# Seven half products instead of eight quarters in both mixers' output projections of a two-layer hybrid decoder trunk

## The chip, the cores and the metric

One core of a Trainium2 chip. The metric is the device time of one execution in microseconds (us), the median of the runs.

## The reference, cut to what matters

512 tokens of 1024 features pass two residual layers; layer 0 mixes by causal pooling, layer 1 by dilated windowed attention. Each layer adds its mixer's output and then a gated feed-forward to the stream x. The part that changes is the last line of each mixer, a product of 512 x 1024 tokens with a 1024 x 1024 weight:

```python
def pool_mixer(h, w_in, w_group, scale, w_out):
    ...
    z = jnp.einsum('bsgc,gce->bsge', p, w_group).reshape(B, S, D_MODEL) * scale
    return jnp.einsum('bsd,de->bse', z, w_out)

def attn_mixer(h, w_qkv, w_out):
    ...
    return jnp.einsum('bse,ed->bsd', merged, w_out)

def reference(...):
    for i in range(DEPTH):
        ...
        x = x + y
        h = rmsnorm(x, norm_ffn[i])
        x = x + swiglu(h, ...)
    return rmsnorm(x, norm_final)
```

## The kernel before, in words

**Precision.** Every float32 operand is split into a high part (a cast to fp32r, done by ACT: whi, bhi, p_hi, h) and a low part (DVE subtracts the cast from the source: wlo, blo, p_lo, h). A product takes three matmuls: high x high, high x low, low x high.

**Weights.** `queue` is one list of all weight blocks in the order of their use. `weights(i)` (L151) loads ahead on SP's queue into the ring wraw, and casts (L171) and subtracts (L175) a few items ahead into whi and wlo, or bhi and blo for items with the pool "b". SP's loads wait, in order, for the splits that free their raw buffer. Items of the feed-forward can be sums of two blocks: the second block is added by an accumulating DMA that POOL issues (L138), or by DVE (L177). One form, "loads" (L180), adds a further block to a raw buffer right after that buffer was split, so that the next item is the running sum.

**Order.** PE's instructions are written in the order in which they run. On ACT, DVE, POOL and SP a scheduler orders them by priority, and `tc.high_priority(URGENT)` puts an instruction ahead. Each engine works through its own list in order, so an instruction that waits holds back all behind it.

**Layer 0.** The windows' matmuls (L562) make p from u in two halves; `group_products(half, banks)` (L570) multiplies p by the group weights, ACT scales the result into the high tokens z_hi (L582) and DVE makes z_lo (L583). `out_projection` (L415) is called once the first half of the groups is there; the second half, 24 matmuls, is a hook behind its first weight block.

**The projection.** Columns 0 to 511 first, in four weight blocks of 256 rows, each for four blocks of 128 tokens (the four banks `four`); then columns 512 to 1023, a token block at a time, with all four weights at hand: 192 matmuls of 128x512 (L425 to L427). Each finished bank is added to x (into_stream, L413's row in the profile), squared and summed by ACT, and multiplied by the next norm's gain, so that the norm of a token block is prepared while the next is multiplied. Before the last token block, blocks 0 and 1 are transposed (L366), and behind it block 2 (L358), for the feed-forward.

**Layer 1.** The attention's heads are merged per 128 features: `merged(t)`, t = 0 to 7, 12 to 24 small matmuls into one of the banks mm, then one DVE multiplication (L1338, L1342) with the heads' weights, which frees the bank, then a split into tokens m_hi, m_lo. The heads' weights come to LB and even_rows by DMAs on POOL's queue (L1250); LB is a ring of three, refilled for t = 5 to 7 when t = 0 to 2 are multiplied. Then the same projection follows.

**Feed-forward.** It already takes seven products per block, with sums of tokens (t1 to t4) and sums of weights; `PLAN` sets its steps.

Of the kernel before, what the change touches and what calls it, by code (L numbers as in the profile page):

```python
# [10 lines left out]
F32 = mybir.dt.float32  # L11
# [6 lines left out]
P = 128  # L18
S = 512
# [50 lines left out]
PLAN = _plan()  # L70
TOKENS = np.arange(S).reshape(J, R).T.reshape(-1)
# [4 lines left out]
def trunk_kernel(ctx: ExitStack, tc: tile.TileContext, x_in, xT, gam, gains, consts, ident_d, w0, wT, w1, wv, w_down, out):  # L76
# [49 lines left out]
    def load(i):  # L126
# [3 lines left out]
        raw = (pools["v"] if item["kind"] == "v" else wraw).tile([P, 1024], F32, name="vraw" if item["kind"] == "v" else "wraw")  # L130
# [20 lines left out]
    def weights(i, split_ahead=4, load_ahead=5, held=0):  # L151

        load_ahead = queue[i].get("ahead", load_ahead)
        for n in range(loaded["w"], min(len(queue), i + load_ahead)):
            if queue[n]["kind"] == "w":
                load(n)
            loaded["w"] = n + 1
        load_sums()
        while len(ready) < min(loaded["w"], i + split_ahead):
            item = queue[len(ready)]  # L160
            if item["kind"] == "v" and "v" not in pools:
                break
# [34 lines left out]
    w_out, wo = (rows_of(wT[i]) for i in range(2))  # L197
    j_grp = [enqueue(w0[8], (4, 2 * P))]
    j_out = [w_out(BY_GROUP[0], 0)]
    j_grp.append(enqueue(w0[9], (4, 2 * P)))  # L200
    j_out += [w_out(BY_GROUP[i], 0) for i in (2, 4, 6)] + [w_out(BY_GROUP[i], 1, pool="b") for i in (0, 2, 4, 6)]
# [58 lines left out]
    j_wo = [wo(2 * i, 0) for i in range(4)] + [wo(2 * i, 1, pool="b") for i in range(4)]  # L260
# [206 lines left out]

    with ExitStack() as pctx:
# [3 lines left out]
        early = [pmm.tile([P, S], F32, name=f"early{i}") for i in range(4)]  # L472
        p_hi, p_lo = (pm.tile([P, NC, S], F32R, name=name) for name in ("p_hi", "p_lo"))
# [96 lines left out]
        def group_products(half, banks):  # L570
            whi, wlo = weights(j_grp[half])
            for gg in range(2):
                g = 3 - (2 * half + gg)
                for m in range(2):
# [6 lines left out]
                    sc = g_sb[:, NC + e : NC + e + 1]  # L581
                    nc.scalar.activation(z_hi[:, e, :], ps, AF.Copy, scale=sc)  # L582
# [3 lines left out]

        for b in range(4):
            u_out(b, 0, early[b])
# [12 lines left out]
        banks = [early[0:2], early[2:4]]  # L601

        def turned_banks():
            return banks.pop(0)

        third = out_projection(j_out, BY_GROUP, z_hi, z_lo, norm, SHIFT, [mm.tile([P, S], F32, name="mm") for _ in range(4)], turned_banks, lambda: group_products(1, early))

    def ffn(layer, norm, third, nxt):
# [8 lines left out]
        with ExitStack() as fctx:  # L617
# [261 lines left out]
            for at, (kind, n, i, *zs) in enumerate(PLAN[:-4]):  # L879
                if at in (0, 2):  # L880
                    b = 2 + at // 2
                    if b == 2:
                        late_banks[b] = third
                        norm.prepare(3, COLS)
                    else:
# [100 lines left out]
    with ExitStack() as actx:  # L986
# [359 lines left out]
        for t in range(8):  # L1346
            cast, rest = merged(t)
# [81 lines left out]
```

## Time and profile before

| | us |
|---|---|
| median of 3 runs (lowest to highest) | 981.42 (980.79 to 981.96) |
| the profiled execution | 980.24 |
| its span, first to last instruction | 978.5 |
| layer 0's projection on PE, with 24 group products and the first transposes | 63.3 to 113.7 |
| layer 1's merged heads and projection on PE | 593 to 647.3 |

Engines: PE is TensorE's matmuls, PEld its weight loads, DVE, ACT, POOL, and SP, which issues loads. A row of a timeline gives start, length, engine, line, operation, out<-in, shape and count (x4: four in a row), and in brackets the idle time before it and what ended that. A row of groups gives count | busy us, mean ns of one | idle time before them. Neighbours on one engine overlap by some 0.1 us, so a queue moves a little faster than the means say.

### The profile page before, as it was taken

How to read it: one execution, taken by the hardware profiler on the slowest of the kernel's cores; microseconds unless marked ns; L12 is line 12 of the kernel's file. 1: busy time of each engine (PE TensorE's matmuls, PEld its weight loads, DVE VectorE, ACT ScalarE, POOL GpSimd, SP SyncE). 2: the span in 40 equal slices, each digit the busy share in tenths (PEclk: the TensorE clock that was granted, in tenths of full speed). 3: DMA queues.
4: the chain of work that ended last, by engine and by line, in shares of the span. 5: the costliest groups of instructions: out<-in, count | busy, mean ns of one | idle time of the engine just before them, and what ended most of it. 6: DMA issues, size and time to landing. Idle time of an engine off the chain costs nothing.

```text
span 978.5 us, 15597 instructions
## 1 busy us (share of the span) xinstructions
PE 970.9 (99%) x6028; PEld 862.6 (88%) x6028; DVE 783.9 (80%) x1083; ACT 575.3 (59%) x903; POOL 124.7 (13%) x124
## 2 busy tenths in 40 slices
PE   9999999999999999999999999999999999999997
PEld 8888899988988999889888899899998998899886
DVE  6475799888888888797897547579988898888876
ACT  6573566655665666574553554366664675567655
POOL 0002010010011111101212124101011101110110
PEclk9999999999999999999999999999999999999999
DMA  9448267479668877555221249627657947987652
GB/s 346 176 157 207 45 187 186 124 200 248 165 151 222 218 201 159 117 193 165 86 79 55 62 137 295 115 59 204 174 145 205 251 111 173 250 213 193 153 134 101
DMA packets 79466, 163.00 MB, mean 167 GB/s; under 512 B 6096, under 2 KB 6480, under 8 KB 79392
## 3 DMA queue, kind: packets, MB, share of 16 engines
q1 hardware_dynamic: 58544, 122.04, 37.6%
q0 software_dynamic: 20560, 39.69, 23.7%
q8 instruction: 47, 0.77, 0.3%
q14 instruction: 27, 0.22, 0.1%
q10 hardware_dynamic: 288, 0.27, 0.1%
HBM read 159.85 MB, written 2.13 MB: 166 GB/s over the span
## 4 chain that ended last, share of the span: by engine, by line
PE 99%; ACT 0%; DVE 0%; issue 0%; ACTq 0%
PE pair L703 32%; PE pair L847 21%; PE p L729 5%; PE mm L264 5%; PE mm L266 4%; PE mm L265 4%; PE pair L729 4%; PE r L729 2%; PE early L515 2%; PE mm L425 2%; PE mm L427 2%; PE mm L426 2%; PE mm L729 1%; PE mm L1297 1%; PE mm L1298 1%; PE mm L1299 1%
## 5 line engine op out<-in xcount | busy, mean ns | idle before, releaser
L175 DVE TENSOR_TENSOR wlo<-wraw,whi 128x1024 fp32r<-128x1024 f32 (+2 forms) x190 | 221.7, 1172 | 65.6 <-ACT whi L171 65.0
L171 ACT CAST whi<-wraw 128x1024 fp32r<-128x1024 f32 (+2 forms) x189 | 184.0, 979 | 138.4 <-PE pair L703 27.8
L171 ACT CAST whi<-vraw 128x1024 fp32r<-128x1024 f32 (+1 forms) x108 | 105.2, 980 | 117.6 <-DVE vraw L177 39.8
L175 DVE TENSOR_TENSOR wlo<-vraw,whi 128x1024 fp32r<-128x1024 f32 (+1 forms) x108 | 121.5, 1133 | 46.2 <-ACT whi L171 46.2
L703 PE MATMUL pair<-h,whi 128*128 128x512 f32 (+1 forms) x640 | 143.2, 349 | 0.0
L703 PEld LDWEIGHTS pair<-h,whi 128*128 128x128 f32 x640 | 109.1, 188 | 13.4
L703 PE MATMUL pair<-t,whi 128*128 128x512 f32 (+1 forms) x512 | 110.6, 337 | 0.0
L847 PE MATMUL pair<-whi,u_hi 128*128 128x512 f32 (+1 forms) x284 | 109.9, 387 | 0.0
L847 PE MATMUL pair<-wlo,u_hi 128*128 128x512 f32 (+1 forms) x284 | 109.9, 387 | 0.0
L847 PE MATMUL pair<-whi,u_lo 128*128 128x512 f32 (+1 forms) x284 | 109.7, 386 | 0.0
L703 PEld LDWEIGHTS pair<-t,whi 128*128 128x128 f32 x512 | 86.1, 190 | 8.4
L703 PE MATMUL pair<-h,wlo 128*128 128x256 f32 x512 | 89.2, 281 | 0.0
L703 PEld LDWEIGHTS pair<-h,wlo 128*128 128x128 f32 x512 | 76.1, 188 | 4.2
L138 POOL DMA_DIRECT2D wraw<-w x22 | 26.6, 1211 | 396.0 <-DMA wraw<-w 123.2
L177 DVE TENSOR_TENSOR vraw<-vraw,wraw 128x1024 f32<-128x1024 f32 (+1 forms) x66 | 75.2, 1139 | 0.7
L703 PE MATMUL pair<-t,wlo 128*128 128x256 f32 x384 | 71.9, 282 | 0.0
L264 PE MATMUL mm<-h,whi 128*128 128x512 f32 (+1 forms) x176 | 64.3, 365 | 0.0
L266 PE MATMUL mm<-h,wlo 128*128 128x512 f32 (+1 forms) x176 | 63.4, 360 | 0.0
L265 PE MATMUL mm<-h,whi 128*128 128x512 f32 (+1 forms) x176 | 63.4, 360 | 0.0
L847 PEld LDWEIGHTS pair<-whi,u_lo 128*128 128x128 f32 x284 | 53.3, 188 | 10.9
L847 PEld LDWEIGHTS pair<-whi,u_hi 128*128 128x128 f32 x284 | 53.4, 188 | 10.4
L847 PEld LDWEIGHTS pair<-wlo,u_hi 128*128 128x128 f32 x284 | 53.4, 188 | 10.2
(363 smaller groups left out, 2021.4 us busy)
## 6 DMA issues: line engine op xcount, KB each, us to landing
wraw<-w SPq DMA_DIRECT2D x116, 512.0 KB, 4.7
wraw<-w_down SPq DMA_DIRECT2D x32, 512.0 KB, 4.2
vraw<-w SPq DMA_DIRECT2D x22, 512.0 KB, 4.8
wraw<-w POOLq DMA_DIRECT2D x22, 512.0 KB, 6.9
vraw<-w POOLq DMA_DIRECT2D x22, 512.0 KB, 9.1
wraw<-wT SPq DMA_DIRECT2D x16, 512.0 KB, 4.4
vraw<-w_down POOLq DMA_DIRECT2D x12, 512.0 KB, 6.5
wraw<-w_down SPq DMA_DIRECT2D x24, 256.0 KB, 3.3
```

What stands on the lines that cost most here:

```text
L138: nc.gpsimd.dma_start(dst, more, accum_op=ALU.add)
L171: nc.scalar.copy(hi[:, :n], raw[:, :n])
L175: nc.vector.tensor_sub(lo[:, :n], raw[:, :n], hi[:, :n].bitcast(F32))
L177: nc.vector.tensor_add(raws[into][:, :n], raws[into][:, :n], raws[more][:, :n])
L264: nc.tensor.matmul(ps, lhsT=whi, rhs=xhi, start=first, stop=False, **kw)
L265: nc.tensor.matmul(ps, lhsT=whi, rhs=xlo, start=False, stop=False, **kw)
L266: nc.tensor.matmul(ps, lhsT=wlo, rhs=xhi, start=False, stop=last, **kw)
L425: nc.tensor.matmul(ps, lhsT=xhi, rhs=w[0][:, k, :], start=first, stop=False)
L426: nc.tensor.matmul(ps, lhsT=xhi, rhs=w[1][:, k, :], start=False, stop=False)
L703: mat = lambda o, w, m, **kw: nc.tensor.matmul(o, lhsT=w, rhs=m, skip_group_check=True, **kw)
L729: nc.tensor.matmul(ps[:, g, :], lhsT=w[:, g, c, :], rhs=right[:, z, c, :], start=i in (0, 1, 3) and g + c + k == 0, stop=c == 3 and k == 2 ...
L847: nc.tensor.matmul(acc(t), lhsT=u, rhs=w, start=first, stop=n == len(places) - 1, skip_group_check=True)
```

## The change

`out_projection` stays in the code; both layers now call `seven_projection`. The tokens are taken as two halves of 256, the weight as 2 x 2 blocks of 512 x 512, and seven products of half the tokens with 512 x 512 weights replace eight: 7 x 24 matmuls of 128x512 instead of 192. They run in the order 0, 1, 2, 5, 4, 3, 6, each in two halves z of the rows.

Weights are 14 items instead of 8: products 0, 3 and 6 take one block, product 4 the sum of two, product 1 the sum of two in a buffer of its own pool "s" (sraw), and products 2 and 5 the same buffer after one further "loads" each (L188 after the change). The 14 are split like the 8 before.

Tokens: `Left` keeps the unsplit tokens (raw, two tiles) and one sum (spare), and splits seven operands ("places") of 128x1024: `first` for product 0, `second` for product 1, `behind` for the others, ahead of what they are used by, all URGENT. In layer 0 product 0's banks are copied by ACT (keep) and product 0 is not added to x by itself.

The feed-forward now transposes block 2 after its first step instead of finding it done. In layer 1 the first feed-forward weights are no longer tied behind the last split of the merged heads, and bhi, blo have 3 buffers instead of 4.

```diff
 def load(i):
+        if item.get("sums"):
+            raw = pools["s"].tile([P, 1024], F32, name="sraw")
+        else: ...

+    def enqueue_seven(w, order, then=None):
+        by = w.rearrange("(k p) c -> p k c", p=P)
+        js = {}
+        for i in SEVEN:
+            for z in range(2):
+                block = lambda m, k: by[:, order[2 * k + z] : order[2 * k + z] + 2, COLS[m]]
+                src = {0: [(0, 0)], 1: [(1, 0), (1, 1)], 3: [(0, 1)], 4: [(0, 0), (1, 0)], 6: [(1, 1)]}.get(i)
+                item = dict(kind="w" if src else "sum", shape=(2, S), rows=True, ahead=8, **({"pool": "b"} if z else {}))
...
+                    item["into"] = js[1][z]
+                if i == 1:
+                    item["sums"] = True
+                if i in (1, 2):
+                    item["loads"] = (js[1][z] if i == 2 else len(queue), block(0, i - 1))

+        def behind(self, i):
+            t, more = self.raw
+            with tc.high_priority(URGENT):
+                if i is None:
+                    self.next_sum(FIRST)
+                    self.split(2, self.spare)
+                    self.split(5, more[:, :, FIRST])
+                    nc.vector.tensor_sub(t[:, :, FIRST], more[:, :, FIRST], t[:, :, FIRST])
+                elif i == 0:
+                    self.split(6, t[:, :, FIRST])
+                elif i == 1:
+                    self.split(3, more[:, :, SECOND])
+                    self.next_sum(SECOND)
+                elif i == 4:
+                    self.split(4, self.spare)

+    def seven_projection(js, left, norm, shift, p, r, q, tps, after_first, keep):
+        accs = {0: p, 1: r, 2: p, 3: q, 4: p, 5: r, 6: p}
+        def operands(i):
+            return [weights(j, split_ahead=6, held=z + (i in (4, 3, 6))) for z, j in enumerate(js[i])]
...
+        products(0, operands(0))
+        after_first()
+        left.behind(0)
...
+        product(1)
+        product(2)
+        product(5)
+        for b in range(2):
+            norm.square(b, 0)
+            norm.gained(b, 0)
+        left.reserve()
+        product(4)
...
+            norm.prepare(b)
+        product(3)
...
+        rests = turned_rows(norm, shift, list(enumerate(tps())))
+        ws = operands(6)
+        rests()
...

 # group_products, layer 0
+                        with tc.high_priority(URGENT):
+                            nc.scalar.activation(raw[half][:, 2 * gg + m, :], ps, AF.Copy, scale=sc)
+                            if half == 0 and m == 1:
+                                left.first(2 * gg)
+                        continue

+            def after_first():
+                group_products(1, early)
+                left.second()
+                left.behind(None)

 # merged(t), layer 1
+                with tc.high_priority(URGENT):
+                    if t in (1, 3):
+                        left.first(t - 1)
+                    elif t == 4:
+                        left.second()
+                    elif t == 7:
+                        left.behind(None)
```

DVE in layer 0, from the second half of product 0's weights on. Before: the low parts of the four blocks of columns 512 to 1023 (blo), then of a weight block, and z_lo of the second groups (L583, out h).

```order
L175 TENSOR_TENSOR blo<-wraw,bhi 128x1024 x4
L175 TENSOR_TENSOR wlo<-wraw,whi 128x1024
L583 SCALAR_TENSOR_TENSOR h<-early_102,g_sb,h 128x512
L583 SCALAR_TENSOR_TENSOR h<-early_103,g_sb,h 128x512
L583 SCALAR_TENSOR_TENSOR h<-early_104,g_sb,h 128x512
L175 TENSOR_TENSOR wlo<-wraw,whi 128x1024
```

Now, from product 1's two halves (the first two rows) to product 2's first half (the last); L526 and L538 are token sums, L423 token splits, L580 adds of product 1's banks to x.

```order
L183 TENSOR_TENSOR wlo<-sraw,whi 128x1024
L183 TENSOR_TENSOR blo<-sraw,bhi 128x1024
L526 SCALAR_TENSOR_TENSOR spare_sum<-spare_sum,raw_107 128x1024
L423 TENSOR_TENSOR h<-raw_107,h 128x1024
L538 TENSOR_TENSOR raw_106<-raw_107,raw_106 128x4x256
L423 TENSOR_TENSOR h<-spare_sum,h 128x1024
L580 TENSOR_TENSOR x<-x,mm 128x512
L423 TENSOR_TENSOR p_lo<-raw_106,p_hi 128x1024
L580 TENSOR_TENSOR x<-x,mm 128x512
L423 TENSOR_TENSOR p_lo<-raw_107,p_hi 128x1024
L526 SCALAR_TENSOR_TENSOR spare_sum<-spare_sum,raw_107 128x1024
L183 TENSOR_TENSOR wlo<-sraw,whi 128x1024
```

Between two weights of the projection there stood at most four 128x512 instructions; between product 1's and product 2's there now stand nine, seven of them of 1024 columns.

DVE in layer 1 at the merged heads. Before: the last weight split, and the multiplications (L1338, L1342) with the token splits (L388).

```order
L175 TENSOR_TENSOR blo<-wraw,bhi 128x1024
L1338 TENSOR_TENSOR o<-mm,LB_5262 128x512
L388 TENSOR_TENSOR h<-o,h 128x512
L1338 TENSOR_TENSOR o<-mm,LB_5263 128x512
L388 TENSOR_TENSOR h<-o,h 128x512
L1338 TENSOR_TENSOR odd_rows<-mm,LB_5264 128x512
```

Now: the raw tokens go to pT's buffer (pT<-mm); the split of product 1's first weight (wlo<-sraw) is the third row.

```order
L1538 TENSOR_TENSOR pT<-mm,LB_5295 128x512
L1538 TENSOR_TENSOR pT<-mm,LB_5296 128x512
L183 TENSOR_TENSOR wlo<-sraw,whi 128x1024
L423 TENSOR_TENSOR h<-pT,h 128x512
L1538 TENSOR_TENSOR pT<-mm,LB_5297 128x512
```

A weight's split has moved between the second and the third multiplication.

POOL's queue in layer 1. Before: the groups' weights (mx<-gw), then the heads' weights in the order of their use.

```order
L1226 DMA mx<-gw 128x1x1 x4
L1244 DMA far<-ropea 64x128
L1250 DMA LB_5262<-far 64x512 x2
L1250 DMA LB_5263<-far 64x512 x2
L1250 DMA LB_5264<-far 64x512 x2
L1250 DMA even_rows<-far 64x512 x4
L1250 DMA LB_5262<-far 64x512 x2
```

Now, with the accumulating DMAs of product 4 (wraw<-wT), product 1 (L144 sraw<-wT) and products 2 and 5 (L188).

```order
L144 DMA wraw<-wT 128x2x512 x2
L1432 DMA far<-ropea 64x128
L1438 DMA LB_5295<-far 64x512 x2
L1438 DMA LB_5296<-far 64x512 x2
L1438 DMA LB_5297<-far 64x512 x2
L1438 DMA even_rows<-far 64x512 x4
L144 DMA sraw<-wT 128x2x512 x2
L1438 DMA LB_5295<-far 64x512 x2
L1438 DMA LB_5296<-far 64x512 x2
L188 DMA sraw<-wT 128x2x512
L1438 DMA LB_5297<-far 64x512 x2
L188 DMA sraw<-wT 128x2x512 x3
```

Two sums stand ahead of the first heads' weights, two ahead of the refills, and one ahead of the last refill.

More of the change, by code (lines that the diff above doesn't have):

```diff
@@ L154, in weights @@
         for n in range(loaded["w"], min(len(queue), i + load_ahead)):
+            if queue[n].get("sums") and "s" not in pools:
+                break
             if queue[n]["kind"] == "w":
@@ L585, in group_products @@
                     )
+        quarters = lambda t: t.rearrange("p a b -> p (a b)").rearrange("p (u k s) -> p u k s", u=4, k=4)
+        if SEVEN_OUT[0]:
+            kept = {u: (z, i) for z, us in ((0, (0, 1, 2, 5)), (1, (6, 3, 4))) for i, u in enumerate(us)}
+            where = [[quarters(t) for t in pair] for pair in ((z_hi, z_lo), (p_hi, p_lo))]
+            left = Left(raw, spare_sum, {u: [t[:, i] for t in where[z]] for u, (z, i) in kept.items()})
         for b in range(4):
@@ L879, in ffn @@
             for at, (kind, n, i, *zs) in enumerate(PLAN[:-4]):
[L880 to L885, printed above, removed]
[L886 to L889 removed]
+                if at == 0:
+                    norm.prepare(3, COLS)
+                if at == (0 if third else 1):
+                    late_banks[2] = third or [by_four(mm.tile()) for _ in range(2)]
+                    if not third:
+                        for half in range(2):
+                            norm.turn(2, half, late_banks[2][half])
+                    late(2, 1)
+                if at == 2:
+                    late_banks[3] = [r_tile(), by_four(mm.tile())]
+                    for half in range(2):
+                        norm.turn(3, half, late_banks[3][half])
+                    late(3, 1)
                 if at in (4, 6, 8):
@@ L1346, in trunk_kernel @@
         for t in range(8):
-            cast, rest = merged(t)
-        for j in (j_wo[-1] + 1, j_wo[-1] + 2):
-            queue[j].update(cast_behind=cast.ins, behind=rest.ins)
+            done = merged(t)
+        if not seven:
+            for j in (j_wo[-1] + 1, j_wo[-1] + 2):
+                queue[j].update(cast_behind=done[0].ins, behind=done[1].ins)
         norm = Norm(2, mp.tile([P, D], F32, name="even_rows"))
@@ L1356, in turned_banks @@
             return [bank() for _ in ROWS]
-        third = out_projection(j_wo, range(NC), m_hi, m_lo, norm, SHIFT, four, turned_banks)
+        if seven:
+            p, q, r, more = four[:2], four[2:], *([mm.tile() for _ in range(2)] for _ in range(2))
+            third = seven_projection(j_wo, left, norm, SHIFT, p, r, q, lambda: (more, r), lambda: None, False)
+            del pools["s"]
+        else:
+            third = out_projection(j_wo, range(NC), m_hi, m_lo, norm, SHIFT, four, turned_banks)
     ffn(1, norm, third, 3)
```

136 lines of the change are left out of this document (119 added, 17 removed).

## The prediction

> **What bounds the kernel now.** I read the page first, then TensorE's waits, then the stretches around both projections, engine by engine.
>
> ```profile
> span 978.5 us, 15597 instructions
> PE 970.9 (99%) x6028; PEld 862.6 (88%) x6028; DVE 783.9 (80%) x1083; ACT 575.3 (59%) x903; POOL 124.7 (13%) x124
> ```
> ```profile
> PE mm L302 <- DVE odd_rows L296: 1.1, 1, 1.1
> ```
>
> TensorE (PE) is busy for 99% of the span, and its one recorded wait is the 1.1 us at the start. So a removed matmul is worth its whole issue time as long as no wait appears, and every us that PE is made to wait is a us lost: there is no slack to absorb it. The span of 978.5 and 1.74 around it make the profiled 980.24 us, 1.18 under the median of 981.42.
>
> Next, how full the engines are that feed PE. Columns: stretch, its length, busy us (instructions) of PE, weight loads, DVE, ACT, POOL, then clock, DMA share, GB/s.
>
> ```profile
> 63.46:86.00 22.54, 22.54 (x100) 18.64 (x100) 14.24 (x17) 11.90 (x16) 4.12 (x4) 1.00 0.79 225
> 86.00:107.00 21.00, 21.00 (x93) 17.11 (x92) 11.54 (x25) 8.38 (x18) 2.04 (x2) 1.00 0.57 110
> 107.00:114.00 7.00, 7.00 (x60) 5.91 (x60) 6.85 (x14) 3.99 (x8) 0.00 (x0) 1.00 0.00 0
> 648.00:660.00 12.00, 12.00 (x104) 12.00 (x103) 11.94 (x19) 8.80 (x15) 0.00 (x0) 1.00 0.27 89
> ```
>
> Layer 0's projection is 63.46 to 114; DVE is busy for 32.6 of its 50.5 us, 17.9 free. Where layer 1's feed-forward starts (648), DVE has nothing free.
>
> **What the change removes.** In both layers 24 of 192 matmuls of 128x512 go.
>
> ```profile
> 63.30 0.45 PE L425 MATMUL mm<-whi,h 128*128 128x512 f32 x1
> 68.84 0.39 PE L264 MATMUL early<-p_hi,whi 128*128 128x512 f32 x1
> 74.28 0.39 PE L425 MATMUL mm<-whi,h 128*128 128x512 f32 x1
> ```
>
> From 63.30 to 68.84 run 24 of them, then 24 of group products to 74.28: 5.5 us for 24. One product of the new scheme takes 5.5 us too. Saving: 2 x 5.5 = 11.0 us.
>
> **What it adds, and the price of each.** Durations:
>
> ```profile
> L175 DVE TENSOR_TENSOR wlo<-wraw,whi 128x1024 fp32r<-128x1024 f32 x156 | 196.9, 1267 | 56.1 <-ACT whi L171 55.4
> 62.49 0.68 ACT L582 ACTIVATE h<-mm,g_sb 128x512 fp32r<-128x512 f32 x1
> 63.07 2.03 ACT L387 CAST p_hi<-early 128x512 fp32r<-128x512 f32 x4
> 64.97 3.92 ACT L171 CAST bhi<-wraw 128x1024 fp32r<-128x1024 f32 x4
> 64.42 2.48 DVE L388 TENSOR_TENSOR p_lo<-early,p_hi 128x512 fp32r<-128x512 f32 x4
> 66.81 4.62 DVE L175 TENSOR_TENSOR blo<-wraw,bhi 128x1024 fp32r<-128x1024 f32 x4
> ```
>
> Queued behind each other (the last two pairs), a 128x1024 costs ACT 0.95 and DVE 1.13 us, a 128x512 0.5 and 0.6. Per projection DVE gets 6 more weight splits (6.8), 7 token places (7.9), 4 token sums (4.5) and at least 2 more flushes (1.2), and loses 8 token splits of 128x512 (4.8): some 15.6 us more. Layer 0 had 17.9 free, less the 5.5 by which it would shorten: 12.4. DVE no longer fits under PE even with nothing waiting.
>
> The operands of products 1, 2 and 5 are one buffer per half, to which POOL's accumulating DMA adds a block each time. Its cost, from the one place where the trace has that chain (layer 0's last down product):
>
> ```profile
> 401.98 3.36 POOL L180 DMA_DIRECT2D vraw<-w_down  x3 [10.88 <-DVE wlo L175]
> DMA to landing us min/median/max: 5.6/7.1/7.8
> 400.35 2.96 DVE L175 TENSOR_TENSOR wlo<-vraw,whi 128x1024 fp32r<-128x1024 f32 x3
> 407.85 1.05 ACT L171 CAST whi<-vraw 128x1024 fp32r<-128x1024 f32 x1 [5.58 <-DMA vraw<-w_down]
> 408.94 1.22 DVE L175 TENSOR_TENSOR wlo<-vraw,whi 128x1024 fp32r<-128x1024 f32 x1 [3.09 <-ACT whi L171]
> 410.38 1.05 ACT L171 CAST whi<-vraw 128x1024 fp32r<-128x1024 f32 x1 [1.48 <-DMA vraw<-w_down]
> wraw<-wT SPq DMA_DIRECT2D x16, 512.0 KB, 4.4
> ```
>
> DVE's first split of the old contents ends at 401.5, POOL issues, ACT casts at 407.85, DVE's new split ends at 410.16: 8.6 us round trip against 5.5 us of product; a second one right behind lands 2.5 us later. The Trainium skill (DMA: Bandwidth & Descriptors, Anatomy of one DMA) fits 2.0 us + bytes/436e3 to such a DMA; estimated from that, 512 KB would land in 3.2 us and 2.4 less in each of the five places below where PE waits for a landing, so the sum would be 12 us smaller. The trace has 5.6 at best, and the sum goes by that.
>
> Layer 0, on the clock of the profile before; PE starts product 0 at 63.3.
>
> *First weights of half two.* ACT now does 128x512 casts of tokens twice, a 128x1024 one, and p_hi, ahead of bhi, which starts at 66.6 where it was 64.97; DVE can begin the first token sum when the last group result is out (62.49 + 0.68 = 63.2) and has 5.3 us of token work ahead of blo: ready at 69.6. PE, after 12 matmuls, wants it at 66.3: 3.3 us lost. If the tokens were split later, 0; with the split of the weights first nothing else moves.
>
> *Product 1.* Loads start when the last window matmul frees the room (63.3), land at 67.7, the sums at 74 and 76.5; splits end by 76 and 79.5. Group products end at 77.6 (63.3 + 3.3 + 5.5 + 5.5), so both are in time, under their cover; without it product 1 would lose 4 us. It ends at 83.2.
>
> *Product 2.* Its sum can be issued at 76 and land at 82 to 84. But its DVE split stands behind the rows shown under the change: counted from the split of product 1's second half (end 79.5), sum 1.2, two token splits and a difference 3.4, flush 0.6, token split 1.1, flush 0.6, token split 1.1, sum 1.2, itself 1.1 = 10.3: ready at 89.8, or 91 since one token split waits for an ACT cast that stands behind the cast of this very weight. PE wants it with its second matmul at 83.4: 7.6 lost. Bounds: 1 (landing at 82, no queue) and 11 (landing after 7.8 us, then what is left of the queue).
>
> *Product 5.* The round trip of 8.6 against 5.5: 3.0 lost (0 to 5). *Norm before the transposes*: two ACT scalings behind product 3's start, 1.0 (0 to 2.5).
>
> *Feed-forward start.* ACT's second cast of t2 now stands behind the cast of a summed weight whose load waits for a DVE sum of the first feed-forward products: 4.4 + 5.6 + 0.95 = 11 us from that sum to the cast. In the old order that weight's load came a product earlier and PE didn't wait. SP's queue adds to it: its loads of the first feed-forward weights stand behind ones that wait for the projection's splits, so all of DVE's lateness is handed on. Between 0 and 11 I take 6, since DVE has no free time there to catch up (the row of 648). The transposes of block 2, moved behind the first step of the feed-forward, cost PE what they cost before, and the two ACT copies of product 0 (0.7 each) lie under the group products.
>
> Layer 0: 3.3 + 7.6 + 3.0 + 1.0 + 6.0 = 20.9 lost.
>
> Layer 1:
>
> ```profile
> 602.23 0.50 PE L425 MATMUL sc<-whi,h 128*128 128x512 f32 x1
> 592.42 1.16 POOL L1250 DMA_DIRECT2D even_rows<-far  x2 [1.04 <-DMA LB<-far]
> 599.07 0.68 DVE L1338 TENSOR_TENSOR odd_rows<-mm,LB 128x512 f32<-128x512 f32 x1
> 607.78 1.07 DVE L1342 TENSOR_TENSOR odd_rows<-mm,LB 128x512 f32<-128x512 f32 x1 [0.68 <-DMA LB<-far]
> ```
>
> *Merged heads.* POOL has two more sums (1.2 each to issue) ahead of these DMAs, and two after even_rows, so product 1's first sum is issued at 596 and lands at 602; its split ends at 604, and stands on DVE ahead of the third multiplication, which was at 599.07 and frees a bank. 4.5 us lost (0 if the sum lands by 598; 8 at the slowest landing and with LB's DMAs between). *Product 2*: the last multiplication moves from 608.85 to 613; behind it stand 12 DVE instructions, 12 us: ready at 625. PE, which began the first product at 602.3, is 4.5 late at 606.8 and wants it two products later, at 617.8: 7.5 lost (3 to 11). *Product 5* 3.0, *norm* 1.0. *Feed-forward start*: as in layer 0, but its sums' loads come earlier, 4.0 (0 to 11). Layer 1: 20.0.
>
> **The clock.** Waits of 7 us and more are new to this kernel, so I looked where PE is idle in the trace, at its ends.
>
> ```profile
> 5.38 1.94 PE L515 MATMUL early<-whi,h 128*128 128x512 f32 x4
> 7.16 1.09 PE L515 MATMUL early<-wlo,h 128*128 128x512 f32 x4
> 971.75 0.28 PE L847 MATMUL pair<-whi,t 128*128 128x256 f32 x1
> 976.00:977.00 1.00, 0.00 (x0) 0.00 (x0) 0.00 (x0) 0.00 (x0) 0.00 (x0) 0.72 0.91 340
> 977.00:978.00 1.00, 0.00 (x0) 0.00 (x0) 0.00 (x0) 0.00 (x0) 0.00 (x0) 0.50 0.00 0
> ```
>
> The granted clock falls to 0.50 at 976.44 (0.72 over that us), 4.4 us after the last matmul; and at the start four 128x512 take 1.94 us until 7.16, then 1.09. So the two waits of 7 to 8 us end with PE at half speed, until 6 us after its return at most: 0 to 3 us each, I take 2, 4.0 in all. The Trainium skill (TensorE: Matmul & The Clock Gate, Part 1) has the gate close after an idle window of about 3.4 us; by that the waits of 4 to 6 us would close it as well, some 6 us more, and the trace's 4.4 us leaves that open.
>
> **Sum.** 20.9 + 20.0 + 4.0 - 11.0 = +33.9: 980.24 + 33.9 = 1014.1, and with the median's 1.18, 1015.
>
> **Rivals.**
> A, forecast: waits as above, 0.55; its own range, with half of the wide bounds either way, 1003 to 1028.
> B, only the waits that the queues' order forces (products 2 and 5, the first blo), while norm, merged heads, feed-forward and clock find cover: 3.3 + 7.6 + 7.5 + 6.0 - 11.0 = +13.4, 995 us. For it: PE waited for none of the feed-forward's sums before. 0.17.
> C, slower still: the new sums meet the loads (DMA share 0.79 in the first stretch) and land after 7.8 instead of 5.6 us in five places, 11 us, or more waits close the clock, up to 6 us: 1021 to 1032. 0.14.
> D, the other side: product 2's split is there when product 1 ends. It decides at 83.4 (and 618 in layer 1): DVE would need the token splits of places 5, 2, 6, 3 done before the group products end, and the sum landed by 81; then product 5 follows within its cover and PE keeps its 99%: 980.24 - 11.0 = 969, 970.5. Against: those splits read the second half's tokens, which ACT finishes only at 78. 0.10.
> E, D with the first stalls left, within 2 us of 981.4: 0.04. That the change does not do what it says I give nothing: the order has 5824 matmuls for 5872.
>
> Less than 0.2% (2 us) a measurement of this kernel hardly tells from no change. Faster 0.10, same 0.04, slower 0.86. The range 994 to 1030 holds A, most of B and most of C, some 0.8.
>
> **What would show it.** Right: PE waits for ACT and DVE of 7 to 8 us at product 2 in both layers, 3 at product 5, about 3 before half two of product 0, a merged-heads wait of 4 to 5, PE busy some 40 us short of the span, a clock under 1.00 right after product 2's waits. Wrong: no PE wait over 2 us in either projection; accumulating DMAs that land in 3 to 4 us; or product 2 waiting for the DMA itself, with DVE idle before its split.

## The result, and the profile after

1034.94 us, median of 5 runs (1031.91 to 1036.68), against 980.79 us (980.37 to 981.96) for the kernel before on the same chip: 1.0544 times as long, 95% interval 1.0519 to 1.0568. The forecast was 1015.0 with a range of 994 to 1030: slower, as forecast, but by 54.1 us and not by 34, outside the range.

The page after, first engine line. Busy time against the span is the first thing to read.

```profile
span 1033.1 us, 15590 instructions
PE 980.3 (95%) x5980; PEld 865.1 (84%) x5980; DVE 816.6 (79%) x1113; ACT 597.8 (58%) x925; POOL 144.5 (14%) x140
```

Two things happened at once. PE stood idle for 1033.1 - 980.3 = 52.8 us where it was 978.5 - 970.9 = 7.6: 45.2 more. And PE is *busy* for 9.4 us more although 48 matmuls, 11.0 us, are gone: the matmuls that are left took 20.4 us longer. 45.2 + 20.4 - 11.0 = 54.6, the difference of the two spans. The second part can't be seen in a list of waits.

Both layers have a like share. The windows from each projection's start to the first down product of its feed-forward, after and then before (columns as in the prediction):

```profile
63.30:217.00 153.70, 132.00 (x845) 118.52 (x845) 122.62 (x164) 91.30 (x130) 19.02 (x16) 0.92 0.64 158
621.00:777.60 156.60, 134.69 (x980) 122.82 (x981) 129.42 (x173) 88.22 (x124) 27.27 (x32) 0.92 0.65 162
```
```profile
63.30:189.90 126.60, 126.56 (x866) 116.45 (x866) 102.75 (x146) 75.23 (x112) 11.85 (x10) 1.00 0.57 150
593.50:723.20 129.70, 129.70 (x1002) 120.56 (x999) 105.17 (x151) 73.19 (x109) 15.05 (x17) 1.00 0.60 156
```

Layer 0 is 27.1 us longer and layer 1 26.9. PE's idle time there is 153.70 - 132.00 = 21.7 and 156.60 - 134.69 = 21.9, and the granted clock is 0.92 where it was 1.00.

TensorE's waits after (us in total, times, longest), where before had one of 1.1 us:

```profile
PE mm L1532 <- DVE pT L1538: 7.9, 1, 7.9
PE mm L571 <- DVE wlo L183: 6.8, 3, 6.0
PE pair L914 <- ACT keep L966: 5.0, 2, 3.1
PE sc L571 <- DVE wlo L183: 4.8, 1, 4.8
PE p L914 <- ACT t L422: 4.7, 1, 4.7
PE mm L393 <- ACT even_rows L387: 3.4, 2, 3.2
```

L571 is a product of the new scheme (mm in layer 0; mm and sc in layer 1), L1532 the merged heads, L914 the feed-forward's first products, L393 the transposes of a token block.

The stretches in which the trace grants half the clock, one window each (the eighth is left out but stands in the sum):

```profile
68.90:72.31 3.41, 3.02 (x7) 2.44 (x8) 0.34 (x1) 0.00 (x0) 1.57 (x2) 0.51 0.67 111
89.39:99.62 10.23, 5.39 (x13) 4.28 (x14) 7.06 (x7) 1.25 (x2) 2.44 (x2) 0.50 0.32 49
150.83:157.65 6.82, 5.04 (x22) 4.75 (x23) 5.20 (x7) 4.16 (x7) 0.00 (x0) 0.51 0.52 179
188.38:191.78 3.40, 3.40 (x18) 3.40 (x17) 2.36 (x2) 1.61 (x3) 1.20 (x1) 0.51 0.88 235
632.11:642.34 10.23, 5.43 (x37) 4.77 (x38) 7.91 (x9) 4.60 (x6) 2.35 (x3) 0.50 0.78 167
656.00:662.83 6.83, 5.29 (x13) 4.17 (x14) 2.62 (x3) 0.00 (x0) 2.42 (x2) 0.51 0.40 67
686.73:690.13 3.40, 3.40 (x16) 2.67 (x13) 3.40 (x8) 1.99 (x5) 2.42 (x2) 0.51 1.06 252
...
sum 47.72, PE 33.91 PEld 29.43 DVE 32.30 ACT 16.93 POOL 12.40; mean PE 4.24 PEld 3.68 DVE 4.04 ACT 2.12 POOL 1.55
```

Eight stretches, 47.7 us, in which PE worked 33.9 us at half speed: 17.0 us lost. (The other 3.4 of the 20.4 I lay to the first matmul behind each wait, 0.50 us where a queued one has 0.39; that was not tried apart.) The prediction counted two of them, product 2's in both layers (89.39 and 656.00). The other six come behind the merged heads' 7.9 us and behind waits of 1.8 to 4.7 us; the first behind two short ones, 0.97 and 1.29 us.

Product 2 of layer 0, the largest wait there. Rows of a timeline: TensorE, POOL, ACT, DVE.

```profile
84.71 0.39 PE L571 MATMUL mm<-bhi,h 128*128 128x512 f32 x1
87.75 0.50 PE L571 MATMUL mm<-whi,h 128*128 128x512 f32 x1 [2.66 <-ACT whi L179]
94.23 0.80 PE L571 MATMUL mm<-wlo,h 128*128 128x512 f32 x1 [5.98 <-DVE wlo L183]
...
68.03 2.44 POOL L144 DMA_DIRECT2D sraw<-wT  x2 [24.52 <-DVE p_lo L423]
76.57 1.20 POOL L188 DMA_DIRECT2D sraw<-wT  x1 [6.11 <-DVE wlo L183]
...
73.91 1.05 ACT L179 CAST whi<-sraw 128x1024 fp32r<-128x1024 f32 x1 [6.46 <-DMA sraw<-wT]
79.94 1.05 ACT L179 CAST bhi<-sraw 128x1024 fp32r<-128x1024 f32 x1 [4.40 <-DMA sraw<-wT]
80.90 0.68 ACT L744 ACTIVATE raw<-early,g_sb 128x512 f32<-128x512 f32 x1
83.08 0.69 ACT L744 ACTIVATE raw<-early,g_sb 128x512 f32<-128x512 f32 x1
...
81.03 1.23 DVE L183 TENSOR_TENSOR blo<-sraw,bhi 128x1024 fp32r<-128x1024 f32 x1 [4.82 <-ACT bhi L179]
83.81 1.22 DVE L526 SCALAR_TENSOR_TENSOR spare_sum<-spare_sum,raw 128x1024 f32<-128x1024 f32 x1 [1.55 <-ACT raw L744]
92.96 1.22 DVE L183 TENSOR_TENSOR wlo<-sraw,whi 128x1024 fp32r<-128x1024 f32 x1
```

Read it from the bottom. wlo for product 2 ends at 94.2, as PE starts it. From 83.81 to 92.96 DVE worked through nine operations without a pause, the queue that the prediction listed. But DVE came to them late: it stood idle for 4.82 us, because ACT stood idle for 4.40 us until the second half of product 1's sum landed, about 6 us after the first (73.9, 79.9) and not 2.5. Behind that cast ACT still had the last group results to scale (80.90 to 83.08), which DVE's token sums wait for. One late landing holds back ACT, then DVE, then PE.

### The profile page after: what moved, and what is told of

Read it like the earlier page. It is cut to its first block, busy times and chain, and to the rows that moved or that the text cites. A ratio compares the mean times of both kernels' runs of the same rounds, so it can differ in the third digit from the quotient of the medians.

```text
span 1033.1 us, 15590 instructions
## 1 busy us (share of the span) xinstructions
PE 980.3 (95%) x5980; PEld 865.1 (84%) x5980; DVE 816.6 (79%) x1113; ACT 597.8 (58%) x925; POOL 144.5 (14%) x140
## 3 DMA queue, kind: packets, MB, share of 16 engines
q0 software_dynamic: 24912, 48.08, 27.3%
## 4 chain that ended last, share of the span: by engine, by line
PE 68%; DMA 5%; DVE 4%; ACT 2%; issue 2%; POOL 0%; POOLq 0%; ACTq 0%; DVEq 0%
PE pair L888 31%; PE pair L1032 20%; PE mm L299 3%; PE mm L301 3%; PE mm L300 3%; PE pair L914 3%; PE p L914 1%; DMA LB<-far 1%; DMA sraw<-wT 1%; DMA far<-ropea 1%; DVE wlo L183 1%; DMA vraw<-w 1%; PE r L914 1%; PE mm L914 1%; ACT e L1224 1%
## 5 line engine op out<-in xcount | busy, mean ns | idle before, releaser
L144 POOL DMA_DIRECT2D wraw<-w x22 | 26.5, 1203 | 311.8 <-DMA wraw<-w 89.6
L1032 PEld LDWEIGHTS pair<-wlo,u_hi 128*128 128x128 f32 x284 | 53.4, 188 | 10.2
```

The lines of the kernel that those rows point to most:

```text
L144: nc.gpsimd.dma_start(dst, more, accum_op=ALU.add)
L1032: nc.tensor.matmul(acc(t), lhsT=u, rhs=w, start=first, stop=n == len(places) - 1, skip_group_check=True)
```

## The experiments

The theory after the result had two halves. *Landings*: the accumulating DMAs come late and, in the order of the queues, hold up ACT and DVE. *Room*: DVE has more work in the projections than fits under PE. And *the clock* multiplies whatever waits there are. The rivals were the one half without the other, the work of one layer alone, and the third block's late transposes. For each run: what it lost against the kernel before, and how that splits by the page into PE's idle time above 7.6 us and PE's busy time above that of its matmuls (970.9, less 5.5 per changed layer).

| run | median us | ratio to before (95%) | idle, us | slower matmuls, us |
|---|---|---|---|---|
| after | 1034.94 | 1.0544 (1.0519 to 1.0568) | 45.2 | 20.4 |
| layer 0 only | 1005.18 | 1.0248 (1.0226 to 1.0270) | 21.6 | 8.7 |
| layer 1 only | 1007.39 | 1.0270 (1.0243 to 1.0296) | 23.6 | 10.6 |
| no weight sums | 1001.58 | 1.0205 (1.0181 to 1.0229) | 21.4 | 10.1 |
| weights before tokens | 1015.01 | 1.0344 (1.0325 to 1.0364) | 30.0 | 14.7 |
| both of these | 991.75 | 1.0113 (1.0098 to 1.0128) | 13.9 | 7.6 |
| and heads first | 1009.21 | 1.0287 (1.0270 to 1.0304) | 25.0 | 15.0 |
| and first blo | 1009.27 | 1.0302 (1.0278 to 1.0327) | 27.3 | 16.9 |
| and product 4 between | 1016.16 | 1.0363 (1.0346 to 1.0380) | 30.6 | 16.5 |
| short token splits | 1005.35 | 1.0246 (1.0229 to 1.0263) | 25.9 | 12.1 |
| all three | 988.83 | 1.0080 (1.0062 to 1.0098) | 13.0 | 8.1 |
| third block inside | 980.04 | 0.9997 (0.9988 to 1.0007) | | |
| splits three times | 991.74 | 1.0121 (1.0106 to 1.0136) | 7.3 | 3.9 |
| splits four times | 1007.31 | 1.0270 (1.0253 to 1.0287) | 22.4 | 8.0 |

The last two columns are those of the profiled execution. In "and first blo" and "splits four times" it took 4.2 and 3.4 us longer than the median, so there they add up to more than the median lost; elsewhere it lay within 2 us of it.

**One layer at a time.**

```diff
-SEVEN_OUT = (True, True)
+SEVEN_OUT = (True, False)    # the first run; (False, True) in the second
```

> Only layer 0 takes seven products. If the two projections cost independently of each other, this shows layer 0's share alone, +27 us (the first down product moves from 189.9 to 217.0 in the traces): 1008. If the loss comes from something that both share (the ring of raw buffers, the order of later loads), the two single changes will not add up to the +54 of both: 995 or less here.

> Only layer 1 takes seven products. Independent costs: +27.5 us, 1008, with the wait of 8 us in the merged heads and of 5 at product 2 as in the trace of both. A shared cause: 995 or less.

24.6 and 26.8 us over the 980.63 of before: 51.3 of the 54.1. The two layers lose nearly independently, and neither carries the result alone.

**No sums of weights.** The operands of products 1, 2, 4 and 5 are plain blocks, so no accumulating DMA is in the projections; matmuls, casts and splits stay.

```diff
-src = {0: [(0, 0)], 1: [(1, 0), (1, 1)], 3: [(0, 1)], 4: [(0, 0), (1, 0)], 6: [(1, 1)]}.get(i)
+src = {0: [(0, 0)], 3: [(0, 1)], 4: [(1, 0)], 6: [(1, 1)]}.get(i, [(1, 0)])
-if i == 1:
-    item["sums"] = True
-if i in (1, 2):
-    item["loads"] = (js[1][z] if i == 2 else len(queue), block(0, i - 1))
```

> Both layers, but every weight of products 1, 2, 4 and 5 is one plainly loaded block; the sums of weight blocks are left out, and with them all 16 new accumulating DMAs and their buffer. Theory of the queues' order: the landing of the sums is only the start of the waits; without them ACT takes the group results at once and the token sums start at 79 instead of 83.8, but product 2's split still stands behind nine DVE instructions: product 2 waits 3 to 4 us instead of 8.6 in layer 0, the merged heads 0 to 1 instead of 7.9, product 5 nothing; some 17 us of waits and 10 of half clock go: 1008. Theory of the DMAs: all waits at the products and the merged heads go, 23 us and 13 of half clock: 998, and product 2 waits for nothing.

33 us less than after. Product 2's wait in layer 0 falls from 8.6 to 0.83 us, and it is now for tokens. The merged heads still wait 3.97. DVE's rows of this run show that the weight no longer stands behind the tokens:

```profile
82.30 1.22 DVE L183 TENSOR_TENSOR wlo<-wraw,whi 128x1024 fp32r<-128x1024 f32 x1 [4.02 <-ACT whi L179]
83.45 1.22 DVE L522 SCALAR_TENSOR_TENSOR spare_sum<-spare_sum,raw 128x1024 f32<-128x1024 f32 x1
```

So the run takes away the landing and, by the scheduler, the bad order with it: landings or order, not landings alone. What stays, 21 us, has no sums at all.

**Weights before tokens.** The sums stay; the token operands that are not needed yet are split behind the weights of products 2 and 5.

```diff
-                    self.split(5, more[:, :, FIRST])   # and its difference, before product 1
-                elif i == 0:
-                    self.split(6, t[:, :, FIRST])
+                elif i == 1:
+                    self.split(5, more[:, :, FIRST])
...
+                elif i == 2:
+                    self.split(6, t[:, :, FIRST])
...
-            left.behind(i)
+            after = {1: js[2][1], 2: js[5][1]}.get(i)
+            with tc.issue_after(done_lo[after].ins) if after else nullcontext():
+                ...
+                    left.behind(i)
```

> Both layers, all computed; only the token splits of places 5, 6 and 3 are issued later, behind product 2's and product 5's weight splits. Theory of the queues' order: product 2's wait falls from 8.6 to about 3 in layer 0 (what is left is the landing) and from 4.8 to under 1 in layer 1; the merged heads keep their 8; 9 us of waits and 4 to 6 of half clock go: 1020. Theory of the DMAs: the wait stays, now for the landing, 1032. Theory that DVE is simply too full: the wait moves to products 5 and 4, where the late token splits are then missing: 1030.

20 us less. TensorE in this run:

```profile
86.14 0.50 PE L573 MATMUL mm<-whi,h 128*128 128x512 f32 x1 [1.72 <-ACT h L423]
97.78 0.50 PE L573 MATMUL mm<-wlo,h 128*128 128x512 f32 x1 [2.82 <-DVE wlo L184]
152.31 0.38 PE L919 MATMUL p<-t,whi 128*128 128x256 f32 x1 [0.93 <-DVE t L424]
622.44 3.68 PE L1537 MATMUL mm<-pT,v 128*64 128x128 f32 x32 [8.06 <-DVE pT L1543]
```

In layer 0 product 2 waits 1.72 and 0.63 where it waited 8.6; product 5 now waits 2.82; and the feed-forward's wait of 4.73 us is 0.93, though nothing was changed there. DVE's queue at product 2 was thus the cause of the lateness later on. In layer 1 the merged heads' wait is as it was, and the norm's rose from 1.84 to 3.80.

**Both of these**, without sums and with the weights ahead.

> e3_no_weight_sums and e4_weights_before_tokens in one: no sums of weight blocks, and the token splits late. Theory of the queues' order: after e3 nothing of product 2's wait is left for the order to remove, so the two gains (33 and 20 us) overlap: 1000. If they were independent causes they would add: 981.

991.75: 43 of the 54 us are gone. If the two edits acted apart, 33 + 20 would be all of it; 10 are shared. The four runs (after, each edit, both) can be read as pairs: taking the sums away is worth 33 us in the old order and 23 in the new (1015.01 to 991.75), and the new order is worth 20 us with the sums and 10 without (1001.58 to 991.75). 11 us over the kernel before are left. The waits left are the first weights of half two (1.94 and 2.22 us), merged heads (3.56), and the feed-forward's start (2.06).

**The clock by itself.** A small kernel in place of the trunk: rows of 60 or 67 equal matmuls, and between them a pause set by ACT copies that the next matmul waits for.

```diff
+    def pause(widths):
+        for w in widths:
+            nc.scalar.copy(seen[:, :w], bank[:, :w])
+    for extra in (0, 7):
+        for widths in PAUSES:
+            pause(widths)
+            multiply(60 + extra)
```

> A kernel of its own that leaves the whole trunk out: groups of 60 or 67 matmuls of 128x512, and between them PE waits for a bank that ACT copies 1 to 16 times (0.6 us each); then short pauses of 1 or 2 copies with only 6, 12 or 24 matmuls between. Theory of the prediction: only a pause of over 4.4 us halves the clock, for up to 6 us after it. Theory from the trace after: the gate looks at the share of busy time in stretches of some 3.4 us, so pauses of 2 to 3 us halve it too, sometimes, and two of 1 us close together can; each time for 3.4 us or a multiple, so each costs 1.7 us or more.

It ran once, 692.99 us. Start, length of the whole row of 60 (then 67) matmuls, and the pause before it:

```profile
70.99 13.90 PE L91 MATMUL bank<-h 128*128 128x512 f32 x60 [1.97 <-ACT seen L95]
87.48 15.36 PE L91 MATMUL bank<-h 128*128 128x512 f32 x60 [2.58 <-ACT seen L95]
106.04 13.89 PE L91 MATMUL bank<-h 128*128 128x512 f32 x60 [3.20 <-ACT seen L95]
187.03 16.66 PE L91 MATMUL bank<-h 128*128 128x512 f32 x60 [6.29 <-ACT seen L95]
237.74 15.32 PE L91 MATMUL bank<-h 128*128 128x512 f32 x60 [10.00 <-ACT seen L95]
...
303.92 15.49 PE L91 MATMUL bank<-h 128*128 128x512 f32 x67 [1.97 <-ACT seen L95]
342.31 17.11 PE L91 MATMUL bank<-h 128*128 128x512 f32 x67 [3.20 <-ACT seen L95]
```

Sixty matmuls take 13.90 us. Behind a pause of 1.97 they still do; behind 2.58 they take 1.46 us more, both times it was tried; behind 3.20 nothing once and 1.62 more once; behind 6.29 2.76 more (1.77 in the row of 67); behind 10.00 only 1.42 more, since part of the slow time passes in the pause (the clock is at half from 230.53 to 240.77, and the row starts at 237.74). So a wait of 2.6 us can cost as much again as half its length, and the 4.4 us that the prediction read at the kernel's end was no threshold.

Why 3.20 us did it only once can be read from the times at which the granted clock changes. In each trace they all lie on one grid of 3.41 us. Two windows of this run's grid (columns as before):

```profile
83.76:87.17 3.41, 1.13 (x5) 0.59 (x4) 0.00 (x0) 2.09 (x4) 0.00 (x0) 1.00 0.00 0
104.24:107.66 3.42, 1.62 (x7) 1.36 (x8) 0.00 (x0) 1.68 (x3) 0.00 (x0) 1.00 0.00 0
```

Of the pause of 2.58 us 2.28 lie in the first window, and half clock follows. The pause of 3.20 us that cost nothing lies across a border of the grid, 1.40 us before 104.24 and 1.80 behind it, and neither window is followed by half clock. Laid over all 16 traces, 4422 windows of the grid began at full clock. The 66 with 1.85 us or more of idle time in them were all followed by half clock, the 4345 with under 1.6 us by none, and of the 11 between by 3. So the theory from the trace after holds: the idle time within one window counts, and one wait can be split by the border or added to the next. Only its price was too high: a stretch cost as little as 1.42 us, not 1.7.

**Heads first.** On top of weights before tokens, in layer 1: product 4's sums go behind the last refill of LB on POOL's queue, and product 1's splits behind the merged heads' sixth and eighth multiplications. The reason for the first is in POOL's rows after:

```profile
605.32 1.27 POOL L144 DMA_DIRECT2D wraw<-wT  x1
608.87 1.22 POOL L144 DMA_DIRECT2D wraw<-wT  x1 [2.29 <-DVE den L1421]
610.23 0.59 POOL L1432 DMA_DIRECT2D far<-ropea  x1
620.47 3.14 POOL L1438 DMA_DIRECT2D LB<-far  x6 [9.66 <-DMA far<-ropea]
...
625.66 2.58 POOL L144 DMA_DIRECT2D sraw<-wT  x2
```
```profile
587.23 3.13 POOL L1250 DMA_DIRECT2D LB<-far  x6 [2.68 <-DMA far<-ropea]
```

The small DMA to far, right behind product 4's two sums, held POOL for 9.66 us; before (second fence) it was 2.68. So all that stands behind far on POOL's queue is issued 7 us later, the heads' weights and then the two sums of product 1 (625.66). What PE waits for in the end is those sums, by ACT's and DVE's rows after:

```profile
633.35 1.04 ACT L179 CAST whi<-sraw 128x1024 fp32r<-128x1024 f32 x1 [11.48 <-DMA sraw<-wT]
634.43 1.23 DVE L183 TENSOR_TENSOR wlo<-sraw,whi 128x1024 fp32r<-128x1024 f32 x1 [8.34 <-ACT whi L179]
```

DVE has done the first two multiplications (624.15 and 625.39) with 0.88 and 0.55 us of waiting for LB. Then it stands idle for 8.34 us ahead of product 1's split, with the third multiplication behind it.

```diff
+            queue[j_wo[1][0]].update(cast_behind=left.casts[1].ins, behind=times[5].ins)
+            queue[j_wo[1][1]].update(cast_behind=left.casts[2].ins, behind=times[7].ins)
+            for j in j_wo[4]:
+                queue[j]["sum_behind"] = sent[-1].ins
```

> As e4_weights_before_tokens, and in layer 1 POOL issues product 4's two sums behind the last refill of the heads' weights, and DVE splits product 1's weights behind the sixth and the last multiplication of the merged heads. Theory of the queues' order: the wait of 8 us in the merged heads goes (far lands 3 us after its issue as before, not 9), with some 3 of half clock: 1004. Theory that the sums' DMAs crowd out the heads' weights anyway: over 4 us of it stays, 1010.

POOL in this run:

```profile
599.65 3.12 POOL L1447 DMA_DIRECT2D LB<-far  x6 [2.72 <-DMA far<-ropea]
```

With the sums behind it, far holds POOL for 2.72 us again. The wait of 8 us is gone (the run moves the sums and the splits at once, so their shares are not told apart), yet the time falls by only 6 us: product 1 now waits 1.89 us for its own weight, products 2 and 5 0.5 to 1.6 each, the norm 2.73 and the transposes of block 2 4.01.

**First blo, and product 4 between.** On top of that, first the first bhi and blo of layer 0 ahead of the token splits, and the group results ahead of the second sum's cast; then also product 4 ahead of product 5, to give the sums more time.

```diff
+        queue[j_out[0][1]]["urgent"] = True
...
-SEVEN = (0, 1, 2, 5, 4, 3, 6)
+SEVEN = (0, 1, 2, 4, 5, 3, 6)    # the second run only
```

> As e7_and_heads_first, and in layer 0 the second half of product 0's weights is split ahead of the windows' last tokens, and ACT takes the second groups' results ahead of the cast of product 1's second sum. Theory of the queues' order: 2.3 us at product 0, 1 at product 1 and 1.7 of half clock go: 1000. If DVE is too full the wait only moves on: 1004.

> As e8_and_first_blo, and product 4 runs between products 2 and 5, so that product 5's sum has 11 us instead of 5.5 for its round trip of 8.6. Theory of the round trip: product 5's waits of 2.8 and 2.3 us go, with 2 to 3 of half clock: 993, unless the norm ahead of the transposes, which now has product 3 alone to hide under, takes it back: 998. If every wait were removed, 970.

No gain, and 7 us worse. The waits moved: in the first run layer 0's at half two of product 0 fell from 2.3 to 1.7 us and product 1's rose from 0.8 to 2.6; with product 4 between, they went to product 4's tokens and weight (2.39 and 2.46), while layer 1's norm, 2.73 before, waited 4.41 and 4.46 in the two runs. Neither gain that was expected came. The orders tried were worth about 26 us and no more.

**Short token splits.** The change, but DVE computes the low part of six of the seven token operands for an eighth of the columns.

```diff
-                split(hi[:, k, :], lo[:, k, :], src[:, k, :])
+                nc.scalar.copy(hi[:, k, :], src[:, k, :])
+                part = slice(0, 256 if u == 4 else 32)
+                nc.vector.tensor_sub(lo[:, k, part], src[:, k, part], hi[:, k, part].bitcast(F32))
```

> The change as it is, but DVE makes the low part of six of the seven token operands for an eighth of the columns only (the rest of those low parts is left out), 6 us of DVE less in each layer, order and sums unchanged. Theory that DVE is too full: each us that DVE gains ahead of product 2's split and ahead of the feed-forward is a us of wait: 4 to 5 at product 2, as much at the feed-forward's start in each layer, and half clock: 1012. Theory of the DMAs: what waits for a landing still waits, 1028.

DVE's busy time falls by 12.1 us (816.6 to 804.5) and the run by 29.6: with the sums and the order as they were, each us of DVE was worth 2.4. Product 2's waits in layer 0 are 0.65 and 2.53; the merged heads' 8.30 us, the wait for product 1's late sum, stays.

**All three**: no sums, weights and heads ahead, short splits.

> No sums of weight blocks, token splits late and short, product 1's and 2's weight splits behind the merged heads' last multiplication. If landing, order and DVE's work are all there is, nearly all waits go and what is left is the norm ahead of the transposes and the first blo: 970 for no wait, 978 with those and one stretch of half clock, so below the kernel before. If something else costs (the norm that starts later, the third block turned inside the feed-forward), 985 or more.

Still 1.0080 times the kernel before. PE is idle for 13.0 us more than before and loses 8.1 to slower matmuls; both stand against 11.0 saved. The waits left are at the first bhi (1.96), the norm (2.67) and the feed-forward's start (2.02 and 2.98), and the profile puts all four down to ACT. This run leaves work out and still doesn't reach the kernel before. DVE has 10.3 us less to do than in the run with both edits (816.3 to 806.0), which brought only 2.9.

**The third block.** Are its transposes inside the feed-forward the part that stays? The kernel before, with only that:

```diff
-        tps = [mm.tile([P, S], F32, name="mm").rearrange("p (j t) -> p j t", j=4) for _ in range(2)]
-        for half in range(2):
-            norm.turn(2, half, tps[half])
-        return tps
```

> The projections of before (eight quarters); of the change only the third token block's transposes inside the feed-forward, after its first step. Where all sums, late and long token splits were gone, 18 us over 970 were left, most of them at the start of the feed-forward. If the later third block makes these by itself: waits of 2 to 5 us at the feed-forward's start in each layer, 986 to 990. If DVE's queue is late there because of the projection's own work: PE waits under 1 us, 981 to 982.

980.04, a ratio of 0.9997: no cost by itself. The waits there in the change are handed on from the projection.

**DVE's work by itself.** Neither sums nor a new order: the kernel before, with the low part of each of the eight projection weights computed three times, or four.

```diff
+                for _ in range(item.get("again", 0)):
+                    nc.vector.tensor_sub(lo[:, :n], raw[:, :n], hi[:, :n].bitcast(F32))
...
+    for j in j_out + j_wo:
+        queue[j]["again"] = 2    # 3 in the second run
```

> The kernel before with its eight quarter products, no sums, no new order; only the low part of each of the eight projection weights is computed three times over on VectorE (16 more operations of about 1.1 us, some 18 us more of VectorE per layer, about what the change adds). Theory, the change loses because VectorE has too little room in the two projections: VectorE's free time in layer 0's stretch of before was some 18 us, so TensorE begins to wait: 2 to 8 us per layer and a few half-clock stretches, 985 to 1000 us in all. Rival, VectorE's room does not matter and only the landings of the summed weights and the order of the work do: no more than 3 us, 980 to 984 us.

> As the run before, with each low part computed four times over (24 more operations, some 27 us more of VectorE per layer, beyond its free time). Theory of VectorE's room: 9 us or more above the run with three, per layer, so 1000 to 1025 us in all. Rival: again no more than 5 us above the kernel before, 980 to 986 us.

11.6 and 27.2 us. The page with three:

```profile
span 989.7 us, 15619 instructions
PE 974.8 (98%) x6028; PEld 865.9 (87%) x6028; DVE 818.4 (83%) x1115; ACT 575.8 (58%) x903; POOL 124.8 (13%) x124
```

DVE is busy for 34.5 us more than before (783.9), a little more than the change adds (32.7), and this costs 11.6 us: 7.3 of waits, at the norm in layer 0 (2.66 and 2.06 us) and at v in layer 1 (2.59), and 3.9 of slower matmuls. Nine more us per layer cost another 15.6; there PE waits for the repeated low parts themselves (10.05 us in layer 0, 5.35 in layer 1), since the repeats also make each weight later, so the second run prices more than room alone. So a full DVE costs time by itself: 17.3 us more per layer did, where layer 0 had 17.9 free; but not 54 us. In the change the projection is also 5.5 us shorter per layer, so its 16.3 us of DVE weigh like 21.8, which lies between the two runs (17.3 and 26.3): by a line through them about 19 us, an estimate. The change lost 65.1 us before its 11.0 of saving. I lay the rest, some 46 us, to the late landings in the queues' order, which stop a DVE that has no time to catch up; that share is a difference and was not measured by itself.

## Why the prediction was wrong

The step that failed is the clock: "So the two waits of 7 to 8 us end with PE at half speed, until 6 us after its return at most: 0 to 3 us each, I take 2, 4.0 in all". Product 2's two waits were priced nearly right: their stretches have 5.4 and 5.3 us of PE work at half speed, so 5.3 lost together. But six more stretches came, five of them behind waits of under 5 us, which the step took to be too short; they lost another 11.6, and the matmuls took 20.4 longer in all. The 4.4 us was one observation at the end of the kernel, taken for a lower bound of what closes the clock; the pauses alone show 2.58 us to do, and by the grid 1.85 us of idle time in one window did each time. At the kernel's end the 4.4 us were 1.0 us at the end of one window and then a whole idle one. Of the 20.7 us between the forecast's difference (33.9) and the spans' (54.6), 16.4 are this term and 4.3 the waits. The Trainium skill (TensorE: Matmul & The Clock Gate, Part 1) has the gate watch free-running windows of 3413 ns; the stretches here, 3.4, 6.8 and 10.2 us, agree with that. Its idle window as the condition for closing would leave out the pauses of 2.58 us, which closed it each time: the measurement decides, and a window need not be idle throughout.

That the waits came out so near in sum (40.9 forecast, 43.6 in the two windows) is in part luck: in the table below four terms are too high by 8.0 us together, and seven too low by 9.8.

The waits, term by term (measured sums from TensorE's rows):

| term | predicted | layer 0 | predicted | layer 1 |
|---|---|---|---|---|
| first bhi, blo; merged heads | 3.3 | 2.3 | 4.5 | 7.9 |
| product 1 | 0 | 0.5 | 0 | 0 |
| product 2 | 7.6 | 8.6 | 7.5 | 4.8 |
| product 5 | 3.0 | 0.8 | 3.0 | 0.9 |
| norm | 1.0 | 1.4 | 1.0 | 2.2 |
| feed-forward start | 6.0 | 7.8 | 4.0 | 5.5 |
| all idle time in the window | 20.9 | 21.7 | 20.0 | 21.9 |

- *Product 2, layer 0*: right in size, and in mechanism: the split of the summed weight behind the token rows on DVE. Moving them took most of the wait away (2.35 us left). The landing ahead of it, of product 1's second sum, was worse than "a second one right behind lands 2.5 us later" (6 us).
- *Merged heads*: right in mechanism, the split of product 1's first weight on DVE ahead of the third multiplication, but 3.4 us longer. The prediction had its sum issued 2.9 us behind the heads' first matmul (596 against 593.12) and landing 6 us later. It was issued 4.1 us behind it (625.66 against 621.60), since POOL was held by far, and landed 7.7 us later (633.35), while the DMA engines' share was 1.08.
- *Product 2, layer 1* and *product 5*: too high (for product 2 its own 625 and 617.8 give 7.2 and not 7.5), since PE itself was later than reckoned, and what was waited for was ready by then. Product 5's round trip in layer 0 took 8.5 us (94.18 to 102.7), as forecast; product 2 took longer than its 5.5. A wait upstream pays for the ones behind it; a sum of terms that are each worked out on the old clock counts some twice.
- *Feed-forward start*: the size was near, and "all of DVE's lateness is handed on" holds in layer 0: the longest wait fell from 4.73 to 0.93 us when only the projection's order was changed. In layer 1 3.0 of 5.5 us stayed in that run. The transposes of block 2 at no cost: confirmed alone; in the change they waited 3.15 us in layer 1, for the norm.
- *Saving*: 24 matmuls take 5.5 us wherever PE doesn't wait, as said. It was real, and paid for six times over.
- *DVE no longer fits*: right (15.6 us more per layer forecast, 16.3 measured), and worth 11.6 us for an added load of that size by itself.

Rival D (DVE in time, faster) and B (only the forced waits, 995) are refuted. C, 1021 to 1032, came nearest: it had the right direction, "more waits close the clock", but at 6 us.

What stays open: the split of the 46 us or so beyond DVE's room between landing time and queue order. The sums' 33 and 23 us are no pure price of landing, since without the sums the scheduler's order changed too, and no single DMA's landing was made faster by itself. ACT's room is an untested rival for what is left when sums and order are mended: it has 22.5 us more to do (575.3 to 597.8), the last waits are put down to it, and no run changed its work alone. Nor did a run change the ring of bhi and blo alone.

## What to carry to other kernels

Where TensorE is busy for 99% of a span, price the operands before the matmuls saved: work on VectorE beyond its free time in that stretch was lost nearly one for one here (18.0 us more, 15.6 us lost), and each late operand stops every queue that it stands in. Then price every wait of more than about 2 us a second time, for the half clock behind it: where waits make up 1.85 us or more of one 3.41 us window, count at least one window at half speed. Short waits close together add up. An operand that is one buffer rewritten by an accumulating DMA needs its whole round trip, with the wait of whoever stands behind it, to fit under one product.

## What the runs showed of the hardware

The granted clock falls to half for stretches of 3.4, 6.8 or 10.2 us, on a grid of 3.41 us. A window of the grid with 1.85 us or more of idle time was always followed by half clock (66 of 66), one with under 1.6 us never (0 of 4345). At half clock, 69 of 70 windows with under 0.6 us of idle time were followed by full clock, and none of the 46 with more. So where a pause falls on the grid matters: a lone pause of 1.97 us never closed the clock in two tries, 2.58 did both times, 3.20 once of twice. Four pauses of 0.73 or 1.35 us in a row with 6 to 24 matmuls between them never closed it, while in the trunk 0.97 and 1.29 us with half a us between them did (1.77 us of them in one window).

The twelve accumulating DMAs into the one buffer, as the page groups them (KB each, us to landing):

```profile
sraw<-wT POOLq DMA_DIRECT2D x12, 512.0 KB, 6.0
```

6.0 us in the median (3.7 to 11.7), where the prediction's chain had 5.6 at best and 7.1 in the median. Of two issued back to back the second was cast 2.6 to 2.8 us after the first in three of four pairs, as the prediction had it. Only product 1's pair in layer 0 took 6 us; the DMA engines' share was 0.99 there (74 to 80 us) and 0.85 to 0.88 between the casts of the others, but that this caused it was not tried. A small DMA behind two accumulating ones held POOL for 9.7 us instead of 2.7.
